# The two ends of a state-space mixer: ScalarE's tables behind the outputs, the last gelus and weights behind the last outputs, three steps for the gated unit's first tiles, three more idle products

## The chip, the cores and the metric

One core of a Trainium2 chip runs the whole step in one launch. The metric is the device time of one execution in microseconds (us); smaller is better. Engines are named as in the profile: PE (TensorE's products), DVE (VectorE), ACT (ScalarE), POOL (GpSimd), SP (the engine whose queue issues most transfers). "1.2 GHz" and "2.4 GHz" are the two levels of TensorE's granted clock, 0.50 and 1.00 in the profile's column PEclk.

## The reference

Two layers over 1024 prompt frames and 64 sample frames, 1024 wide, float32. Layer 0 is windowed attention with a gated convolution behind it, layer 1 the state-space mixer with a gated convolution behind it. Only the mixer and what joins it matter here:

```python
u = h.reshape(b, n_blk, blk, N_GROUPS, GROUP_SIZE)          # h = rms_norm(x), 64 groups of 16
xr, xi = einsum('blgi,gpi->blgp', u, bbr), einsum('blgi,gpi->blgp', u, bbi)
_, _, sr, si = lax.associative_scan(_affine_combine, (ar, ai, xr, xi), axis=1)
y = einsum('blgp,gip->blgi', sr, cr) - einsum('blgp,gip->blgi', si, ci)
y = y + d_skip * h
z = gelu(y)
ag = z @ w_glu + b_glu                                       # 1024 -> 2048, the gated unit
out = ag[..., :D_MODEL] * sigmoid(ag[..., D_MODEL:])
x = x + rms_norm(out, g_post)
```

## The kernel before

**The mixer's loop** (`ssm`, L1190 to L1355). The 64 groups are 32 pairs. A batch holds two pairs (the first two and the last two batches hold one), 18 batches in all. A batch goes through four stages, a generator each, and `staged(..., oldest=True)` steps four batches at once, the oldest first. Stage 1: PE multiplies the inputs `U` by the pair's weights `pm` into PSUM tile `p1` (L1243); ACT makes two tables that DVE will need, `sc` (L1251, sines with both signs) and `rd` (L1253, decay times a mask). Stage 2: DVE forms the scan's input from `p1`, the cosines in `pm` and `sc` (L1270, L1275, L1276). Stage 3: DVE scans with `rd` (L1287) and turns the result back (L1290, L1291). Stage 4: PE adds the output products into PSUM tiles `p3` (L1299 from `U`, L1305 from the scan); ACT copies them to `ys` (L1313) and the last states to `fin` (L1316). `p3` has four buffers, two batches' worth; `rd` has two, so the next but one table waits for a scan.

**Column tiles.** Four pairs make one column tile `kt` of 128 channels, eight in all. When its `ys` is full, ACT's queue writes it to memory (`yd`, L1320), SP reads it back transposed (`yf`, L1325), ACT takes the gelu (`z`, L1334 and L1337) and rounds it (`zh`, L1343), DVE forms the remainder (`zl`, L1347). The gelu is held behind the outputs issued so far (`order`, a hint to the scheduler that adds no semaphore). Gelus of tiles 0 to 6 come two further steps after the transfer, that of tile 7 comes at once.

**Weights.** `split_unit` (L211) splits a loaded 128x1024 weight tile into `whl`: ACT rounds it (L214), DVE forms the remainder (L215). The gated unit's weights are loaded ahead through two `raw` buffers, two units ahead of use. u1 to u6 below are the first six: u1 and u2 are needed by its first three tiles, u3 and u4 by the next three, u5 and u6 after that.

**The gated unit** (L1383 to L1411). A tile is (m, b): output columns m, frame block b of 384, 384 and 320 frames. It needs `pb` and `pa`, each 8 column tiles of three products (`mm3`, L218). `pb` and `pa` lie in PSUM where the loop's tiles lay, so the first product waits until ACT has read the last `p3`. Each tile is one generator with two steps: the products of column tiles 0 to 6, then column tile 7, the sigmoid and the gate. The first three tiles (m = 0) all take their first step, then their second. `beside()` runs behind each step and prepares sums of the next layer's weights (`sj`, L1365 to L1373, transfers on POOL's queue).

**The loop's beginning.** `ssm_norm` for the last block forms the norm of its frames; `fill` (L224) keeps PE at work there with products that nobody reads, named `idle` (L1147).

What stands where on an engine is set by a scheduler from program order and the hints of `order`; the rows under "The change" are its result.

Of the kernel before, what the change touches and what calls it, by code (L numbers as in the profile page):

```python
# [8 lines left out]
F32 = mybir.dt.float32  # L9
F32R = mybir.dt.float32r  # L10
I32 = mybir.dt.int32
AF = mybir.ActivationFunctionType
# [3 lines left out]
P = 128  # L16
D = 1024
KD = 8
# [22 lines left out]
OW, OKT, OC, OCO, OSI, PRM = 0, 256, 512, 768, 906, 1044  # L41


class Core:
# [133 lines left out]
    def load_unit(self, src):  # L178
# [30 lines left out]
        return self.split_unit(raw)  # L209

    def split_unit(self, raw):  # L211
        nc = self.nc
        w = self.big([P, 2, D], "whl")
        nc.scalar.activation(w[:, 0], raw, AF.Copy)  # L214
        nc.vector.tensor_sub(w[:, 1], raw, w[:, 0].bitcast(F32))  # L215
        return w
# [17 lines left out]
    def rstd(self, src, n, tag, root, bcast=True, first=False, alt=None, adder=None, fine=False):  # L234
        nc = self.nc
        adder = adder or nc.vector
        acc = None
# [24 lines left out]
        for i, c in enumerate(cuts):  # L262
            nc.tensor.matmul(st[:, i:i + 1], acc[:, 0, c:c + P], self.ones, start=True, stop=True)
        v = self.small.tile([P, 4, 4], F32, name="nv" + tag, bufs=3)
# [877 lines left out]
    def ssm_norm(self, xt, b):  # L1142
# [3 lines left out]
        if b == 2:  # L1146
            self.fill(self.mm_ps("idle"), 7, 512, self.last_tr)  # L1147
        ps, r = self.rstd(xt, n, "sqa" if b == 2 else "sqb", True, bcast=b < 2, alt=1 - b % 2, adder=nc.gpsimd if b == 0 else None)
# [12 lines left out]
        if b < 2:  # L1161
            nc.scalar.activation(self.rn[:, 384 * b:384 * b + 384], ps[:, :n], AF.Copy)
            return
        ex = self.ex
        for i, c in enumerate(range(0, n, P)):
            c = min(c, n - P) // 8
            nc.vector.tensor_scalar(ex[:, 16 * i:16 * i + 16], self.dsel, r[:, i:i + 1], None, op0=ALU.mult)
            nc.tensor.matmul(ps[:, c:c + 16], self.lsel, ex[:, 16 * i:16 * i + 16], start=True, stop=True)
        nc.scalar.activation(self.rs[:, 0:32], ps[:, :32], AF.Copy)
# [20 lines left out]
    def ssm(self, after):  # L1190
# [4 lines left out]
        with tc.tile_pool(name="ss", bufs=1) as sp:  # L1195
# [36 lines left out]
            def batch(qs):  # L1232
# [17 lines left out]
                for c in range(2):  # L1250
                    nc.scalar.activation(sc[:, :, c], pm[:, :, OSI:PRM], AF.Copy, scale=(1.0, -1.0)[c])  # L1251
                for e, q in enumerate(qs):
                    nc.scalar.activation(rd[:, e], mask[:, None, :].to_broadcast([P, 2, 138]), AF.Copy, scale=self.rho[:, q:q + 1])  # L1253
                if qs[-1] == 31:
# [63 lines left out]
                if qs[-1] % 4 == 3:  # L1318
# [10 lines left out]
                    if kt < 7:  # L1329
                        yield  # L1330
                        yield
                    z = self.t4([P, T], "z")
                    yv = yf.rearrange("p t c -> p c t")
# [16 lines left out]
            scans, ends = [], []  # L1350
            self.staged([batch(x) for x in [[0], [1]] + [[q, q + 1] for q in range(2, 30, 2)] + [[30], [31]]], oldest=True)
            fo = sp.tile([P, P], F32, name="fo")
            nc.vector.tensor_add(fo, *(fin[:, i].rearrange("p q c s -> p (q c s)") for i in range(2)))
# [30 lines left out]
        with self.boundary():  # L1384
            def tile_(m, b):
                t0, n = BLK[b]
                if m not in ws:
                    ws[m] = self.unit(("w_glu", m)), self.unit(("w_glu", m + KD))
                if m == 0:
                    y[b] = self.bt(self.yp, b, "y")  # L1390
                pa, pb = self.mm_ps("pa"), self.mm_ps("pb")

                def products(ks):
                    for ps, w in ((pb, ws[m][1]), (pa, ws[m][0])):
                        for k in ks:
                            self.mm3(ps[:, :n], w, slice(k * P, (k + 1) * P), zh[b][:, k], zl[b][:, k], k == 0, k == KD - 1)
                products(range(KD - 1))
                yield
# [8 lines left out]

            order = [tile_(m, b) for m, b in self.tail_order(KD, 3)]
            for x in order[:3] * 2 + [x for x in order[3:] for _ in range(2)]:
                next(x)  # L1410
                beside()  # L1411
# [161 lines left out]
```

## Time and profile before

| | us |
|---|---|
| three runs, median (lowest to highest) | 2277.55 (2268.62 to 2286.29) |
| the profiled execution | 2263.99 |
| its span, from first to last instruction | 2262.2 |
| PE busy in the span | 2200.3 (97%) |
| DVE / ACT / POOL busy | 1687.2 / 1019.6 / 418.0 |

The mixer's loop runs from about 1198 to 1305 us of the span; the gated unit follows until about 1508. In the page's 40 slices PE shows 9 nearly everywhere and 8 in the three slices of the loop. A busy PE is not a PE at its peak, since products are pipelined and slower at 1.2 GHz. In the timeline a row gives start, duration, engine, line, operation, tiles, a count (x2 for two alike, merged), and in brackets the idle time of that engine ahead of it with what ended it.

### The profile page before, as it was taken

To read this page: it belongs to the slowest core of one execution; us is meant where nothing else is said; L and a number is where in the kernel's file an instruction comes from. 1 tells how busy PE (TensorE), PEld (TensorE's weight loads), DVE (VectorE), ACT (ScalarE), POOL (GpSimd) and SP (SyncE) were. 2 spreads that over 40 slices of the span, in tenths; PEclk is the share of its full clock that TensorE was granted. 3 is DMA by queue.
4 is the path that set the end of the run, shared out by engine and by line. 5 is a ranking of instruction groups with operands and counts; after the bars stand their busy time and mean duration, and the time that the engine had idled before them with its cause. 6 is when DMAs were issued, how large, how long until landed. Compare 5 with 4: busy or idle time off the path is not lost. (4 is left out here: it accounts for less than half of the span.)

```text
span 2262.2 us, 36054 instructions
## 1 busy us (share of the span) xinstructions
PE 2200.3 (97%) x13869; PEld 2125.5 (94%) x13869; DVE 1687.2 (75%) x2954; ACT 1019.6 (45%) x1839; POOL 418.0 (18%) x474
## 2 busy tenths in 40 slices
PE   9999999999999999999998889999999999999997
PEld 8987789999999999999986689999999999999997
DVE  8677647989877877767758845588997787676764
ACT  5255747422333342555545632253544444345543
POOL 5322004200042414000200035352011011100000
PEclk9999999999999999999998899999999999999999
DMA  5100024655345565887649778752266677568772
GB/s 196 37 21 29 14 68 150 240 190 200 121 138 186 185 208 178 269 272 234 232 159 347 250 249 296 262 166 72 87 220 224 227 276 260 201 236 291 230 255 99
DMA packets 208124, 428.48 MB, mean 189 GB/s; under 512 B 23312, under 2 KB 114224, under 8 KB 205008
## 3 DMA queue, kind: packets, MB, share of 16 engines
q1 hardware_dynamic: 175648, 326.56, 43.4%
q0 software_dynamic: 23984, 95.12, 11.5%
q10 hardware_dynamic: 8320, 4.49, 0.8%
q8 instruction: 109, 1.79, 0.3%
q14 instruction: 63, 0.52, 0.1%
HBM read 297.75 MB, written 128.37 MB: 188 GB/s over the span
## 5 line engine op out<-in xcount | busy, mean ns | idle before, releaser
L220 PE MATMUL mm<-hl,whl 128*128 128x384 f32 (+1 forms) x1960 | 645.0, 329 | 5.9 <-DVE u L517 2.9
L222 PE MATMUL mm<-hh,whl 128*128 128x384 f32 (+1 forms) x1960 | 642.4, 329 | 2.3 <-DVE whl L215 2.3
L221 PE MATMUL mm<-hh,whl 128*128 128x384 f32 (+1 forms) x1960 | 643.6, 328 | 0.0
L220 PEld LDWEIGHTS mm<-hl,whl 128*128 128x128 f32 x1960 | 369.5, 189 | 8.6 <-DVE u L517 3.6
L222 PEld LDWEIGHTS mm<-hh,whl 128*128 128x128 f32 x1960 | 369.4, 189 | 2.9 <-DVE whl L215 2.9
L221 PEld LDWEIGHTS mm<-hh,whl 128*128 128x128 f32 x1960 | 369.9, 189 | 0.0
L214 ACT ACTIVATE whl<-raw 128x1024 fp32r<-128x1024 f32 x202 | 212.9, 1058 | 327.3 <-PE mm L222 170.9
L215 DVE TENSOR_TENSOR whl<-raw,whl 128x1024 fp32r<-128x1024 f32 x202 | 255.3, 1268 | 101.1 <-ACT whl L214 98.0
L220 PE MATMUL mm<-gt,whl 128*128 128x384 f32 (+1 forms) x968 | 317.7, 329 | 4.6 <-ACT whl L214 1.8
L222 PE MATMUL mm<-gt,whl 128*128 128x384 f32 (+1 forms) x968 | 316.3, 327 | 0.7 <-DVE whl L215 0.7
L221 PE MATMUL mm<-gt,whl 128*128 128x384 f32 (+1 forms) x968 | 316.5, 327 | 0.0
L220 PEld LDWEIGHTS mm<-gt,whl 128*128 128x128 f32 x968 | 182.3, 188 | 6.1 <-ACT whl L214 2.1
L222 PEld LDWEIGHTS mm<-gt,whl 128*128 128x128 f32 x968 | 182.1, 188 | 1.0 <-DVE whl L215 1.0
L221 PEld LDWEIGHTS mm<-gt,whl 128*128 128x128 f32 x968 | 182.4, 189 | 0.0
L194 DVE TENSOR_TENSOR whl<-raw,whl 128x1024 fp32r<-128x1024 f32 x84 | 94.7, 1134 | 72.0 <-ACT whl L193 71.3
L193 ACT ACTIVATE whl<-raw 128x1024 fp32r<-128x1024 f32 x84 | 82.6, 987 | 123.6 <-DMA raw<-sd 55.0
L416 ACT ACTIVATE t<-u,ppt 128x1090 f32<-128x1090 f32 x88 | 114.2, 1298 | 49.8 <-DVE u L518 25.1
L417 DVE SCALAR_TENSOR_TENSOR t<-u,ppt,t 128x1090 f32<-128x1090 f32 x88 | 123.6, 1407 | 8.4 <-ACT t L416 7.8
L418 DVE SCALAR_TENSOR_TENSOR t<-u,ppt,t 128x1090 f32<-128x1090 f32 x88 | 123.4, 1403 | 0.4
L408 DVE TENSOR_TENSOR u<-rb,mm 128x384 f32<-128x384 f32 (+1 forms) x164 | 80.3, 503 | 20.7 <-PE mm L222 16.0
L328 POOL TENSOR_TENSOR y<-y,xl 128x768 f32<-128x768 f32 (+1 forms) x16 | 30.7, 1918 | 349.0 <-DVE y L325 285.6
L560 DVE TENSOR_TENSOR gt<-gr,gt 128x768 fp32r<-128x768 f32 (+2 forms) x106 | 90.4, 881 | 5.6 <-ACT gt L559 5.1
(390 smaller groups left out, 4180.4 us busy)
## 6 DMA issues: line engine op xcount, KB each, us to landing
raw<-in_w_up SPq DMA_DIRECT2D x88, 512.0 KB, 4.2
raw<-in_w_down SPq DMA_DIRECT2D x74, 512.0 KB, 4.3
raw<-sd SPq DMA_DIRECT2D x40, 512.0 KB, 4.3
sj<-in_w_up POOLq DMA_DIRECT2D x68, 256.0 KB, 6.1
su<-sj POOLq DMA_DIRECT2D x34, 512.0 KB, 5.9
raw<-su SPq DMA_DIRECT2D x34, 512.0 KB, 4.8
pm<-prm SPq DMA_DIRECT2D x32, 522.0 KB, 7.1
gr<-td SPq DMA_DIRECT2D x40, 384.0 KB, 6.0
```

What stands on the lines that cost most here:

```text
L193: nc.scalar.activation(w[:, 0], raw, AF.Copy)
L194: nc.vector.tensor_sub(w[:, 1], raw, w[:, 0].bitcast(F32))
L214: nc.scalar.activation(w[:, 0], raw, AF.Copy)
L215: nc.vector.tensor_sub(w[:, 1], raw, w[:, 0].bitcast(F32))
L220: nc.tensor.matmul(out, w[:, 0, sl], xl, start=start, stop=False)
L221: nc.tensor.matmul(out, w[:, 0, sl], xh, start=False, stop=False)
L222: self.last_mm = nc.tensor.matmul(out, w[:, 1, sl], xh, start=False, stop=stop)
L408: nc.vector.tensor_mul(u[:, t0 + 2:t0 + 2 + np_], rb[:, t0:t0 + np_], ps[:, :np_])
L416: nc.scalar.activation(t, u[:, 0:T + 2], AF.Identity, bias=cb(m), scale=cw(0, m))
L417: nc.vector.scalar_tensor_tensor(t, u[:, 1:T + 3], cw(1, m), t, op0=ALU.mult, op1=ALU.add)
L418: self.last_conv = nc.vector.scalar_tensor_tensor(t, u[:, 2:T + 4], cw(2, m), t, op0=ALU.mult, op1=ALU.add)
L560: nc.vector.tensor_sub(x[:, 1, u], raw, x[:, 0, u].bitcast(F32))
```

## The change

Five edits; the arithmetic on the data stays as it is:

1. Each `sc` and `rd` is ordered behind the output copy issued last (`out[0]`), in program order that of three batches earlier.
2. `split_unit` can be ordered: after the loop `behind` holds the last output copy (for ACT's half) and the last L1291 (for DVE's half). It holds for the four units that are split until m = 1 is opened, u3 to u6.
3. Column tile 6 takes one more step between transfer and gelu, column tile 7 two, so both gelus fall behind the last output copies.
4. The m = 0 tiles take three steps: column tiles 0 to 5, then 6, then 7. All three take the first step before anything else, without `beside()`.
5. Eight instead of seven idle products of 512 columns ahead of the norm's sums, one more of 512 behind them (`last_st`), and one of 256 behind the three `sel` products.

```diff
+    behind = ()
     def split_unit(self, raw):
-        nc.scalar.activation(w[:, 0], raw, AF.Copy)
-        nc.vector.tensor_sub(w[:, 1], raw, w[:, 0].bitcast(F32))
+        x = nc.scalar.activation(w[:, 0], raw, AF.Copy), nc.vector.tensor_sub(w[:, 1], raw, w[:, 0].bitcast(F32))
+        for u, v in zip(x, self.behind):
+            self.order(u, v)
...
-            self.fill(self.mm_ps("idle"), 7, 512, self.last_tr)
+            idle = self.mm_ps("idle")
+            self.fill(idle, 8, 512, self.last_tr)
...
+        self.fill(idle, 1, 512, self.last_st)
         for i, c in enumerate(range(0, n, P)):
...
+        self.fill(idle, 1, 256, x)
...
                 for c in range(2):
-                    nc.scalar.activation(sc[:, :, c], pm[:, :, OSI:PRM], AF.Copy, scale=(1.0, -1.0)[c])
+                    x = nc.scalar.activation(sc[:, :, c], pm[:, :, OSI:PRM], AF.Copy, scale=(1.0, -1.0)[c])
+                    if out[0]:
+                        self.order(x, out[0])
                 for e, q in enumerate(qs):
-                    nc.scalar.activation(rd[:, e], ..., AF.Copy, scale=self.rho[:, q:q + 1])
+                    x = nc.scalar.activation(rd[:, e], ..., AF.Copy, scale=self.rho[:, q:q + 1])
+                    if out[0]:
+                        self.order(x, out[0])
...
                     if kt < 7:
                         yield
                         yield
+                    if kt == 6:
+                        yield
+                    if kt == 7:
+                        yield
+                        yield
                     z = self.t4([P, T], "z")
...
+            self.behind = out[0], ends[-1]
...
                     ws[m] = self.unit(("w_glu", m)), self.unit(("w_glu", m + KD))
+                    if m:
+                        self.behind = ()
...
-                products(range(KD - 1))
+                k0 = 0
+                if m == 0:
+                    k0 = KD - 2
+                    products(range(k0))
+                    yield
+                products(range(k0, KD - 1))
                 yield
                 products([KD - 1])
...
+            for x in order[:3]:
+                next(x)
             for x in order[:3] * 2 + [x for x in order[3:] for _ in range(2)]:
```

ACT, the middle of the loop. p3_11901 and p3_11902 are the output of the batch of pairs 8 and 9, sc_11951 and rd_11952 the tables of pairs 14 and 15, sc_12010 and rd_12011 those of pairs 16 and 17. Before:

```order
L1253 ACTIVATE rd_11952<-mask_11569,rho_291 128x276 x2
L1320 DMA yd_11535<-ys_11796 128x8x137
L1334 ACT_TABLE_LOAD
L1334 ACTIVATE z_11888<-yf_11744 128x1024
L1337 ACTIVATE z_11888<-yf_11744 128x64
L1251 ACTIVATE sc_11951<-pm_11745 128x2x138 x2
L1343 ACTIVATE zh_11891<-z_11888 128x384
L1343 ACTIVATE zh_11894<-z_11888 128x384
L1343 ACTIVATE zh_11897<-z_11888 128x320
L1251 ACTIVATE sc_12010<-pm_11801 128x2x138 x2
L1253 ACTIVATE rd_12011<-mask_11569,rho_291 128x276 x2
L1313 ACTIVATE ys_11924<-p3_11901 128x2x137
```

Of the change (the same tiles have numbers higher by 3, lines of the new file: L1323 is the output copy, L1257 `sc`, L1261 `rd`, L1330 `yd`, L1350 `z`):

```order
L1330 DMA yd_11538<-ys_11799 128x8x137
L1350 ACT_TABLE_LOAD
L1350 ACTIVATE z_11891<-yf_11747 128x1024
L1353 ACTIVATE z_11891<-yf_11747 128x64
L1359 ACTIVATE zh_11894<-z_11891 128x384
L1359 ACTIVATE zh_11897<-z_11891 128x384
L1359 ACTIVATE zh_11900<-z_11891 128x320
L1323 ACTIVATE ys_11927<-p3_11904 128x2x137
L1323 ACTIVATE ys_11927<-p3_11905 128x2x137
L1326 COPY fin_11571<-wk_11810 128x8 x2
L1257 ACTIVATE sc_11954<-pm_11748 128x2x138 x2
L1261 ACTIVATE rd_11955<-mask_11572,rho_291 128x276 x2
```

The output copy of pairs 8 and 9 stood behind the tables of both later batches; now it stands ahead of both. This repeats in every round from pairs 8 on.

DVE, the last batches. L1287 (128x552, then two of 128x276) is the scan, L215 a weight split. Before:

```order
L215 TENSOR_TENSOR whl<-raw,whl 128x1024
L1291 TENSOR_TENSOR wk<-wk,sc 128x552
L1270 TENSOR_TENSOR wk<-pm,p_12420 128x2x137
L1275 TENSOR_TENSOR wk<-sc,p_12420 128x2x137
L1276 TENSOR_TENSOR wk<-wk 128x2x137
L1287 SCALAR_TENSOR_TENSOR wk<-rd,wk 128x276
L1290 TENSOR_TENSOR wk<-wk,pm 128x276
L1291 TENSOR_TENSOR wk<-wk,sc 128x276
L1270 TENSOR_TENSOR wk<-pm,p_12471 128x2x137
L1275 TENSOR_TENSOR wk<-sc,p_12471 128x2x137
L215 TENSOR_TENSOR whl<-raw,whl 128x1024
L1276 TENSOR_TENSOR wk<-wk 128x2x137
```

Of the change (L216 is the split, L1301 the old L1291, L1280 the old L1270, L1285 the old L1275, L1286 the old L1276, L1297 the scan):

```order
L1301 TENSOR_TENSOR wk<-wk,sc 128x552
L1280 TENSOR_TENSOR wk<-pm,p_12423 128x2x137
L1285 TENSOR_TENSOR wk<-sc,p_12423 128x2x137
L216 TENSOR_TENSOR whl<-raw,whl 128x1024
L1286 TENSOR_TENSOR wk<-wk 128x2x137
L1297 SCALAR_TENSOR_TENSOR wk<-rd,wk 128x276
L1300 TENSOR_TENSOR wk<-wk,pm 128x276
L1301 TENSOR_TENSOR wk<-wk,sc 128x276
L1280 TENSOR_TENSOR wk<-pm,p_12474 128x2x137
L1285 TENSOR_TENSOR wk<-sc,p_12474 128x2x137
L1286 TENSOR_TENSOR wk<-wk 128x2x137
L1297 SCALAR_TENSOR_TENSOR wk<-rd,wk 128x276
```

One split of the three (u3) has left the last batches; u2's has moved by three instructions and stays among them.

ACT, the hand-over to the gated unit. p_12562 and p_12563 are the last output. Before:

```order
L1334 ACTIVATE z<-yf 128x1024
L1337 ACTIVATE z<-yf 128x64
L214 ACTIVATE whl<-raw 128x1024
L1343 ACTIVATE zh<-z 128x384 x2
L1343 ACTIVATE zh<-z 128x320
L1313 ACTIVATE ys<-p_12562 128x137
L1313 ACTIVATE ys<-p_12563 128x137
L1316 COPY fin<-wk 128x4 x2
L214 ACTIVATE whl<-raw 128x1024
L1320 DMA yd<-ys 128x8x137
L1334 ACTIVATE z<-yf 128x1024
```

Of the change (p_12559 and p_12560 are the last output):

```order
L1323 ACTIVATE ys<-p_12559 128x137
L1323 ACTIVATE ys<-p_12560 128x137
L1326 COPY fin<-wk 128x4 x2
L216 ACTIVATE whl<-raw 128x1024 x2
L1330 DMA yd<-ys 128x8x137
L1350 ACTIVATE z<-yf 128x1024
L1353 ACTIVATE z<-yf 128x64
L1359 ACTIVATE zh<-z 128x384 x2
L1359 ACTIVATE zh<-z 128x320
L216 ACTIVATE whl<-raw 128x1024
L1350 ACTIVATE z<-yf 128x1024
```

The gelu of column tile 6 and one split stood ahead of the last output copy; both now stand behind it, and two splits stand between it and the transfer of column tile 7. On SP's queue the weight load of u6 now stands behind the read-back of column tile 7; before, those of u5 to u8 all stood ahead of it.

## Rows read from the trace of the kernel before

**Rows 1.** Windows: span, PE, PEld, DVE, ACT, POOL busy, clock, DMA share, GB/s.

```profile
1250.00:1260.00 10.00, 9.09 (x107) 7.47 (x106) 9.21 (x13) 5.75 (x19) 0.29 (x2) 1.00 0.75 265
1300.00:1310.00 10.00, 5.34 (x54) 4.26 (x52) 5.57 (x10) 6.90 (x16) 0.00 (x0) 0.84 0.52 166
```

**Rows 2.** Waits of DVE in 1203 to 1292: total us, times, longest.

```profile
DVE zl L1347 <- ACT zh L1343: 5.8, 4, 2.9
DVE whl L215 <- ACT whl L214: 2.0, 1, 2.0
DVE wk L1270 <- ACT fin L1316: 0.5, 2, 0.2
```

**Rows 3.** Waits of PE in the same stretch, same columns.

```profile
PE p L1299 <- ACT ys L1313: 8.2, 5, 2.4
```

**Rows 4.** Timeline of DVE in the loop: two scans, the first wait.

```profile
1214.69 1.31 DVE L1287 TENSOR_TENSOR_SCAN wk<-rd,wk 128x552 f32<-128x552 f32 x1
1219.68 1.31 DVE L1287 TENSOR_TENSOR_SCAN wk<-rd,wk 128x552 f32<-128x552 f32 x1
1238.03 1.03 DVE L1347 TENSOR_TENSOR zl<-z,zh 128x384 fp32r<-128x384 f32 x2 [2.91 <-ACT zh L1343]
```

**Rows 5.** Timeline of all engines, one round of the loop.

```profile
1272.92 2.07 ACT L1334 ACTIVATE z<-yf 128x1024 f32<-128x1024 f32 x1 [0.25 <-ACT fin L1316]
1275.10 0.74 ACT L1251 ACTIVATE sc<-pm 128x276 f32<-128x276 f32 x2
1275.17 1.20 PE L1305 MATMUL p<-wk,pm 64*128 64x137 f32 x16
1278.57 0.94 ACT L1253 ACTIVATE rd<-mask,rho 128x276 f32<-128x276 f32 x2 [1.54 <-DVE wk L1287]
1279.42 0.66 ACT L1313 ACTIVATE ys<-p 128x274 f32<-128x274 f32 x2
1279.85 1.11 PE L1299 MATMUL p<-U,pm 128*128 128x137 f32 x4 [2.39 <-ACT ys L1313]
```

**Rows 6.** Timeline of all engines, the last batches and the hand-over.

```profile
1296.01 1.74 PE L1305 MATMUL p<-wk,pm 64*128 64x137 f32 x12 [0.86 <-DVE wk L1291]
1299.55 1.22 DVE L215 TENSOR_TENSOR whl<-raw,whl 128x1024 fp32r<-128x1024 f32 x1
1304.14 1.20 PE L1305 MATMUL p<-wk,pm 64*128 64x137 f32 x16
1305.68 2.03 ACT L1334 ACTIVATE z<-yf 128x1024 f32<-128x1024 f32 x1 [1.87 <-DMA yf<-yd]
1310.52 0.44 ACT L1313 ACTIVATE ys<-p 128x137 f32<-128x137 f32 x2
1311.00 0.69 PE L220 MATMUL pb<-zl,whl 128*128 128x384 f32 x1 [5.66 <-ACT ys L1313]
```

**Rows 7.** Windows, columns as in Rows 1: the gated unit's first products.

```profile
1311.00:1314.00 3.00, 3.00 (x9) 3.00 (x10) 2.36 (x5) 1.09 (x3) 1.46 (x3) 0.50 0.73 164
1314.00:1324.00 10.00, 10.00 (x58) 10.00 (x57) 0.00 (x0) 0.00 (x0) 3.34 (x5) 0.98 1.06 282
```

**Rows 8.** Timeline of ACT: column tile 7 and the first sigmoid.

```profile
1310.98 0.37 ACTq L1320 DMA_DIRECT2D yd<-ys  x1
1324.68 2.15 ACT L1334 ACTIVATE z<-yf 128x1024 f32<-128x1024 f32 x1 [12.59 <-DMA yf<-yd]
1334.18 0.58 ACT L1402 ACTIVATE sg<-pb,ppt 128x384 f32<-128x384 f32 x1 [4.64 <-PE pb L222]
```

**Rows 9.** Timeline of DVE: the last remainder.

```profile
1327.49 1.43 DVE L1347 TENSOR_TENSOR zl<-z,zh 128x384 fp32r<-128x384 f32 x3 [14.13 <-ACT zh L1343]
```

**Rows 10.** DMA issues in 1200 to 1345: count, KB each, median us to landing.

```profile
pm<-prm SPq DMA_DIRECT2D x26, 522.0 KB, 7.4
yd<-ys ACTq DMA_DIRECT2D x8, 548.0 KB, 8.6
```

**Rows 11.** Timeline of POOL at the loop's beginning.

```profile
1201.65 0.19 POOL L1274 COPY wk<-h 128x2 f32<-128x2 f32 x1 [5.18 <-DMA h<-in_s_h]
```

More of the change, by code (lines that the diff above doesn't have):

```diff
@@ L262, in rstd @@
         for i, c in enumerate(cuts):
-            nc.tensor.matmul(st[:, i:i + 1], acc[:, 0, c:c + P], self.ones, start=True, stop=True)
+            self.last_st = nc.tensor.matmul(st[:, i:i + 1], acc[:, 0, c:c + P], self.ones, start=True, stop=True)
         v = self.small.tile([P, 4, 4], F32, name="nv" + tag, bufs=3)
@@ L1167, in ssm_norm @@
             nc.vector.tensor_scalar(ex[:, 16 * i:16 * i + 16], self.dsel, r[:, i:i + 1], None, op0=ALU.mult)
-            nc.tensor.matmul(ps[:, c:c + 16], self.lsel, ex[:, 16 * i:16 * i + 16], start=True, stop=True)
+            x = nc.tensor.matmul(ps[:, c:c + 16], self.lsel, ex[:, 16 * i:16 * i + 16], start=True, stop=True)
+        self.fill(idle, 1, 256, x)
         nc.scalar.activation(self.rs[:, 0:32], ps[:, :32], AF.Copy)
@@ L1250, in batch @@
                 for c in range(2):
-                    nc.scalar.activation(sc[:, :, c], pm[:, :, OSI:PRM], AF.Copy, scale=(1.0, -1.0)[c])
+                    x = nc.scalar.activation(sc[:, :, c], pm[:, :, OSI:PRM], AF.Copy, scale=(1.0, -1.0)[c])
+                    if out[0]:
+                        self.order(x, out[0])
                 for e, q in enumerate(qs):
-                    nc.scalar.activation(rd[:, e], mask[:, None, :].to_broadcast([P, 2, 138]), AF.Copy, scale=self.rho[:, q:q + 1])
+                    x = nc.scalar.activation(rd[:, e], mask[:, None, :].to_broadcast([P, 2, 138]), AF.Copy, scale=self.rho[:, q:q + 1])
+                    if out[0]:
+                        self.order(x, out[0])
                 if qs[-1] == 31:
```

## The prediction

> **What bounds the kernel now.** Over the whole span PE is busy 97%, so the windows of 10 us show where it isn't: only in the mixer's loop and behind it. In 1250 to 1260 DVE is busy 9.21 of 10 and PE 9.09; in 1300 to 1310 PE is busy 5.34 and DVE 5.57, so there nobody works at the bound [rows 1]. That last stretch and the loop are two different cases, and I read them apart.
>
> *The loop.* The timeline of DVE shows a round: from one scan to the next 4.99 us without a gap [rows 4]. DVE is the pace. What the loop loses is DVE's idle time, and the waits of DVE in 1203 to 1292 name it: 5.8 us, in four pieces, for ACT's `zh` ahead of the remainder `zl`, 2.0 us for ACT's half of a weight split, 0.5 us for `fin` [rows 2]. PE's own wait, 8.2 us for ACT's `ys` [rows 3], is on PE's side and is not added: DVE doesn't stop for it.
>
> Why is ACT late, at 6 busy us in 10? The timeline of one round shows it: `rd` waits 1.54 us for DVE's scan, `ys` stands behind it, and PE waits 2.39 us for that `ys` [rows 5]. ACT works in order. As the order of before shows, the output copy of pairs 8 and 9 stands behind the tables of pairs 16 and 17, and the second `rd` of these can't start before a scan one round later. So outputs, the writes of full column tiles, and the gelus behind them all run about a round late.
>
> *The hand-over.* The loop's last products start at 1304.14 and take 1.20. The last `ys` starts at 1310.52, and the gated unit's first product at 1311.00, after 5.66 us of idle PE. In between ACT waits 1.87 us for the read-back of column tile 6, takes its gelu and splits a weight [rows 6]. None of that is needed for the first product but the last `ys`. Behind the gap PE runs at 1.2 GHz: 9 products in 3.00 us, against 58 in 10 us afterwards [rows 7].
>
> **The change part by part.** The sum is made against the profiled execution, 2263.99 us (span 2262.2). It lies 13.6 below the median of the three runs, 2277.55, so the forecast is the saving taken off the median.
>
> *Tables behind outputs.* Nothing is added on ACT; the copies move ahead. Where does DVE's idle time go?
> - The first `zl` wait, 2.91 us [rows 4], is column tile 0, whose gelu waits for its transfer in either order. Between nothing and 0.6 (the `sc` pair of 0.74 [rows 5] that stood between gelu and `zh` is gone, but `yd` may go out up to 0.6 later): I take 0.3.
> - The other three `zl` waits, 5.8 - 2.9 = 2.9 us, and the 0.5 for `fin` [rows 2]: outputs, writes and gelus come up to a round (5 us) earlier, each wait was under 2 us. Bounds 0 (transfers set the pace instead) and 3.4: I take 3.4.
> - The split of u1 waits 2.0 us [rows 2] behind the gelu of column tile 4, which comes earlier by the same: 2.0, bounds 0 and 2.0.
>
> New waits this could make: `sc` now stands behind `ys` three batches older. From the turned-back scan on, that chain is two runs of L1305 at 1.20 and L1299 between them at up to 1.11, `ys` 0.66, `sc` 0.74 [rows 5]: 4.9 us. DVE needs that `sc` two rounds later, 2 x 4.99 = 10.0 [rows 4]. With a gelu and its `zh` and `zl` in between (1324.68 to 1328.92, 4.2 us [rows 8, 9]) 0.9 us is left. Price taken: nothing.
>
> *Splits behind the last outputs.* The split of u3, 1.22 us on DVE, stood in the last batches, and PE waited there for DVE (0.86 in one row) [rows 6]. It now follows the last batch: 1.1 us, since DVE's neighbouring rows overlap by about 0.1; bounds 0 and 1.2. The splits of u2 and u1 stay. What is late next: u3 and u4 are needed by the second three tiles, over 20 us later; no cost.
>
> *Gelus 6 and 7 behind the last `ys`.* The 5.66 us of idle PE [rows 6] shrink to what lies between `ys` and the first product, 1311.00 - 1310.52 = 0.5: a saving of 5.1, bounds 4 (`ys` itself waits for one more copy) and 5.2.
>
> *The clock.* Without that gap the first ten products should run at 2.4 GHz: 3.35 us shrink to 10 x 0.172 = 1.7 [rows 7], 1.6 saved. Bounds 0 (PE still pauses between the last batches, 0.86 us and more [rows 6], and could enter the gated unit at the slow level) and 1.6; as the loop's last products at 1304.14 run 16 in 1.20, as fast as in the loop's middle [rows 5, 6], I take 1.6. The Trainium skill ("TensorE: Matmul & The Clock Gate", Part 1: The HAM clock gate) says that the slow level is the default and that activity lifts it; the trace agrees, 0.50 behind the gap and 0.98 in the next window. By that rule alone the extra idle products would also be worth something, as follows.
>
> *Idle products.* They fill PE's pauses around the last norm. Little can come of it: the loop's first sum waits for POOL's copy of the start state, which waits for its transfer until 1201.65 [rows 11], whatever PE does. Bounds: 0.5 lost (a 512-column product at the slow level ahead of the `sel` products) and 0.5 gained: I take 0.
>
> *Three steps for m = 0.* PE does 3 x 36 products before it needs column tile 6 and 3 x 6 more before 7: 126 x 0.172 = 21.7 us of cover from the hand-over on, as many as before. Column tile 7's way, from the issue of `yd` to its gelu, takes 1324.68 - 1310.98 = 13.7 us, and to the end of the last `zl` 4.2 more [rows 8, 9]: 17.9. Its `yd` goes out 0.1 to 2.5 us after the hand-over now, as two splits stand ahead of it on ACT (about 1.1 each). So it is ready after 18.0 to 20.4, before the cover ends at 21.7; no cost, upper bound 4 if the transfers land late. On SP the read-back now stands ahead of u6's load; u6 is needed by the third three tiles, some 30 us later.
>
> Sum: 0.3 + 3.4 + 2.0 + 1.1 + 5.1 + 1.6 = 13.5 us saved. Profiled: 2264.0 - 13.5 = 2250.5. From the median: 2277.6 - 13.5 = 2264.
>
> **The rivals.**
>
> *Only the hand-over gains* (2270). The loop keeps its pace because transfers set it: `pm` loads take 7.4 us and `yd` writes 8.6 to land at the median [rows 10], and the gelu waits for both legs of a column tile's way. For it: column tile 0's gelu does wait for its transfer. Against it: the DMA share is 0.75 in 1250 to 1260 [rows 1], so there is room. Saved are 1.1 + 5.1 + 1.6 = 7.8. The Trainium skill ("DMA: Bandwidth & Descriptors", Issuing engines are not separate DMA queues) says that transfers of all queues run on the same 16 engines and interleave; that is a rule against this change, as an earlier `yd` on ACT's queue then takes its bandwidth from SP's `pm` loads. The rows show neither.
>
> *Column tile 7 becomes the wait* (2268). The weight sums' transfers start with the hand-over too and collide with `yd`. If the way takes 4 us more than the margin, PE stands idle 4 us before its last 18 products: 13.5 - 4 = 9.5 saved. Before, sg started 5.3 us after the last `zl` ended (1327.49 + 1.43) [rows 8, 9], so the way had room; now the margin is 1.3 to 3.7.
>
> *Tables become the wait, slower* (2288). In rounds with a gelu 0.9 us is left between `sc` and DVE's use of it. If the read-back lands over 0.9 us after ACT gets to the gelu, ACT stands, and now `ys`, `sc` and `rd` stand behind it. At 6 column tiles inside the loop and 4 us each that is 24 us against 13.5; it turns slower than before at 0.9 + 13.5/6 = 3.2 us of delay per tile. For it: the one such wait that rows show, 1.87 us [rows 6]. Against it: writes go out earlier as well, so read-backs land earlier.
>
> **How the numbers follow.** Chances: forecast 0.57, only the hand-over 0.23, column tile 7 0.15, tables 0.05. All but the last lie between 2264 and 2270. The runs of before spread from 2268.62 to 2286.29, some 9 us to either side, which is wider than the cases; the saving's own bounds run from 4 (clock, loop and u3 all at nothing) to 15. So the range is 2246 to 2281: 2264 less 18 (a low run, the profiled execution was 13.6 under its median, and a full saving), and 2270 plus 11. About 1% is what a measurement of this kernel can tell from no change, 22.8 us here; the forecast is 0.6%. Faster by more needs the saving and a low run together: 0.17. Slower by more needs the tables' case at its worst: 0.03. The rest, 0.80, lies within.
>
> **What would show it.** Right: the wait of the gated unit's first product under 1 us and its first ten products at 2.4 GHz; DVE's waits for `zh` in the loop at about 2.6 us in one piece; no wait of PE for `ys` inside the loop; the last scan-to-scan distance shorter by one split; the first sigmoid about 13 us earlier. Wrong: new waits of DVE's L1275 for `sc`, of ACT's `z` for the read-back in most rounds, or of PE for `zl` before its last 18 products of m = 0.

## The result, and the profile of the changed kernel

The changed kernel took 2260.79 us at the median of six runs (2254.65 to 2264.88), the kernel before 2276.97 in six (2268.62 to 2286.29): a ratio of 0.9929, with a 95% interval from 0.9902 to 0.9956. Two further measurements of the same kernel gave 0.9951 (0.9937 to 0.9964) and 0.9939 (0.9922 to 0.9955). By medians these are 16.2, 12.2 and 15.3 us saved. The forecast was 13.5.

The three intervals stand for 10.0 to 22.3, 8.2 to 14.3 and 10.2 to 17.7 us saved. All of them hold the forecast, none holds "only the hand-over" (7.8), and one holds the rival with column tile 7 (9.5). Which part of the change gave how much has to be read from the traces.

The two profiled executions laid side by side don't show it: the span of before was 2262.2 us, that of the change 2263.1. They are single executions, and the stages that the change doesn't touch differ by more than the saving. The mixer has to be read on a clock of its own. I start it at ScalarE's copy of the last block's norm (`sel`, 128x8), behind which the loop begins. Timeline of ACT, before:

```profile
1198.26 0.16 ACT L1170 ACTIVATE sel<-pr 128x8 f32<-128x8 f32 x1
```

and of the change, with the first sigmoid:

```profile
1203.50 0.16 ACT L1176 ACTIVATE sel<-pr 128x8 f32<-128x8 f32 x1
1330.80 0.58 ACT L1427 ACTIVATE sg<-pb,ppt 128x384 f32<-128x384 f32 x1 [5.07 <-PE pb L225]
```

The change reached the mixer 5.24 us later; in its two further executions `sel` came at 1200.02 and 1196.23, in the second one of before at 1206.20, so this is scatter. From `sel` to the first sigmoid it took 1330.80 - 1203.50 = 127.30 us, before 1334.18 [rows 8] - 1198.26 = 135.92: 8.6 us less. With the further profiled executions of both kernels (the runs e1, e2 and e12 below), cut at the same five places:

| us | before | before, e1 | change | change, e2 | change, e12 | mean saved |
|---|---|---|---|---|---|---|
| `sel` to first scan | 4.38 | 4.09 | 4.09 | 4.14 | 4.24 | 0.1 |
| first to last scan | 99.33 | 101.76 | 95.89 | 95.17 | 93.53 | 5.7 |
| last scan to last products | 2.17 | 2.32 | 3.94 | 2.32 | 2.20 | -0.6 |
| last products to gated unit | 6.86 | 7.35 | 1.75 | 2.01 | 2.13 | 5.1 |
| its first product to first sigmoid | 23.18 | 23.17 | 21.63 | 21.68 | 21.63 | 1.5 |
| sum | 135.92 | 138.69 | 127.30 | 125.32 | 123.73 | 11.9 |

The terms of the forecast were 6.8 for the loop with u3's split, 5.1 and 1.6. The mixer's own clock shows 11.9 us saved on the mean; where the timed runs show more, the rows don't say where it comes from. The 3.94 of the change's first execution is the clock. Timeline of PE, and the window behind its first row with the columns of [rows 1]:

```profile
1297.59 0.51 PE L1315 MATMUL p<-wk,pm 64*128 64x137 f32 x4 [2.05 <-DVE wk L1300]
```

```profile
1298.27:1305.22 6.95, 6.95 (x39) 5.66 (x39) 6.64 (x14) 4.33 (x9) 0.41 (x3) 0.51 0.99 235
```

Behind 2.05 us without work PE ran the last batches at 1.2 GHz (0.51), without a gap, so that its products set the end there. In e2 and e12 most of these products ran at 2.4 GHz, in e2 behind a pause as long (2.06 us), and the way took 2.2 to 2.3 us. The slow form isn't a single case: it came again in e5 and e9 (3.53 and 3.82 us).

**The hand-over.** Timeline of the change, PE and ACT, where [rows 6] showed 5.66 us of idle PE:

```profile
1307.42 1.20 PE L1315 MATMUL p<-wk,pm 64*128 64x137 f32 x16
1308.65 0.46 ACT L1323 ACTIVATE ys<-p 128x137 f32<-128x137 f32 x2 [1.56 <-PE p L1315]
1309.17 0.44 PE L223 MATMUL pb<-zl,whl 128*128 128x384 f32 x1 [0.55 <-ACT ys L1323]
```

The last copy now waits for nothing but its products, and the gated unit starts 0.55 us behind it. The windows behind, with the columns of [rows 7]:

```profile
1309.17:1312.17 3.00, 3.00 (x17) 3.00 (x18) 2.18 (x3) 3.00 (x5) 0.55 (x1) 1.00 0.71 199
1312.17:1322.17 10.00, 10.00 (x60) 10.00 (x59) 3.41 (x6) 6.64 (x11) 4.25 (x6) 1.00 0.87 247
```

The granted clock is 1.00 (2.4 GHz) from the start, where it was 0.50; 17 products fit into 3 us, where it was 9.

**Column tile 7.** ACT and DVE of the change:

```profile
1319.10 2.14 ACT L1350 ACTIVATE z<-yf 128x1024 f32<-128x1024 f32 x1 [1.73 <-DMA yf<-yd]
1321.90 1.43 DVE L1363 TENSOR_TENSOR zl<-z,zh 128x384 fp32r<-128x384 f32 x3 [3.27 <-ACT zh L1359]
```

The last remainder ends at 1321.90 + 1.43 = 1323.33, 14.2 us after the first product. In PE's timeline the first product of column tile 7 starts at 1330.07, 20.9 us after the first product, behind 126 others (108 come ahead of column tile 6). PE never waited.

**The loop.** Waits of DVE and of PE in 1208 to 1297, the same stretch on the mixer's clock as in [rows 2, 3]:

```profile
DVE zl L1363 <- ACT zh L1359: 7.5, 2, 4.2
```

```profile
PE p L1249 <- DMA pm<-prm: 4.8, 5, 2.1
PE p L1309 <- ACT ys L1323: 0.5, 1, 0.5
```

PE's wait for `ys` is down from 8.2 us to 0.5 (what is left is for `pm` transfers; that wait was 2.1 us before, 4.1 in e1), and DVE no longer waits for the weight split or `fin`. But DVE's wait for `zh`, 5.8 us in four pieces before, is now 7.5 in two. Timeline of DVE:

```profile
1243.53 1.03 DVE L1363 TENSOR_TENSOR zl<-z,zh 128x384 fp32r<-128x384 f32 x2 [3.32 <-ACT zh L1359]
1249.78 1.31 DVE L1297 TENSOR_TENSOR_SCAN wk<-rd,wk 128x552 f32<-128x552 f32 x1
1259.19 1.03 DVE L1363 TENSOR_TENSOR zl<-z,zh 128x384 fp32r<-128x384 f32 x2 [4.19 <-ACT zh L1359]
1260.13 1.30 DVE L1297 TENSOR_TENSOR_SCAN wk<-rd,wk 128x552 f32<-128x552 f32 x1
```

The round of column tile 1 takes 10.35 us from scan to scan. Before it took 7.38. ACT, and then SP's queue, show why:

```profile
1247.13 0.37 ACTq L1330 DMA_DIRECT2D yd<-ys  x1
1256.51 2.04 ACT L1350 ACTIVATE z<-yf 128x1024 f32<-128x1024 f32 x1 [7.72 <-DMA yf<-yd]
```

```profile
1247.57 0.33 SPq L1335 DMA_DIRECT2D yf<-yd  x1
```

The write of column tile 2 goes out at 1247.13, the read-back of tile 1 at 1247.57, and its gelu can start only at 1256.51, 8.9 us later. ACT stands for 7.7 of them, with the next outputs behind the gelu. Before, in the order SP, ACT, ACT, by rows of its timeline:

```profile
1242.57 0.33 SPq L1325 DMA_DIRECT2D yf<-yd  x1
1247.17 0.37 ACTq L1320 DMA_DIRECT2D yd<-ys  x1
1247.58 2.08 ACT L1334 ACTIVATE z<-yf 128x1024 f32<-128x1024 f32 x1 [0.25 <-ACT fin L1316]
```

There the read-back of tile 1 had landed in 5.0 us or less, and the write of tile 2 went out 4.6 us behind it. The read-back itself starts at the same time on the mixer's clock (1242.57 - 1198.26 = 44.3, and 1247.57 - 1203.50 = 44.1); what has moved is the write beside it.

Why doesn't it start earlier? On SP's queue it waits for the write of tile 1 to land. That write, on ACT's queue, before and in the change:

```profile
1231.42 0.37 ACTq L1320 DMA_DIRECT2D yd<-ys  x1
```

```profile
1233.04 0.37 ACTq L1330 DMA_DIRECT2D yd<-ys  x1
```

On the mixer's clock it goes out 3.6 us earlier in the change (29.5 against 33.2), but the read-back follows 14.5 us behind it instead of 11.2. In the further executions this is 13.0 and 13.4 us (e2, e12) against 11.7 (e1). So the earlier write of tile 1 gained next to nothing: its read-back starts 43.4 to 44.1 us behind `sel` in the change, 44.3 and 44.6 before.

### The profile page after: what moved, and what is told of

Read it like the earlier page. It is cut to its first block, busy times and chain, and to the rows that moved or that the text cites. A ratio compares the mean times of both kernels' runs of the same rounds, so it can differ in the third digit from the quotient of the medians.

```text
span 2263.1 us, 36074 instructions
## 1 busy us (share of the span) xinstructions
PE 2201.7 (97%) x13875; PEld 2122.4 (94%) x13875; DVE 1688.5 (75%) x2954; ACT 1019.2 (45%) x1839; POOL 415.2 (18%) x474
## 5 line engine op out<-in xcount | busy, mean ns | idle before, releaser
L216 ACT ACTIVATE whl<-raw 128x1024 fp32r<-128x1024 f32 x202 | 212.9, 1058 | 339.1 <-PE mm L225 176.4
L216 DVE TENSOR_TENSOR whl<-raw,whl 128x1024 fp32r<-128x1024 f32 x202 | 254.4, 1263 | 96.7 <-ACT whl L216 96.2
L223 PEld LDWEIGHTS mm<-gt,whl 128*128 128x128 f32 x968 | 182.9, 189 | 10.5 <-DVE y L613 4.9
L562 ACT ACTIVATE gt<-gr 128x768 fp32r<-128x768 f32 (+2 forms) x106 | 78.3, 771 | 39.5 <-DMA gr<-gd 30.2
```

The costliest lines, as they stand in the source:

```text
L216: x = nc.scalar.activation(w[:, 0], raw, AF.Copy), nc.vector.tensor_sub(w[:, 1], raw, w[:, 0].bitcast(F32))
L223: nc.tensor.matmul(out, w[:, 0, sl], xl, start=start, stop=False)
L562: nc.scalar.activation(x[:, 0, u], raw, AF.Copy)
```

## The experiments

My theory was the prediction's sum, loop included. The rivals: that only the hand-over gains, and a collision of the earlier write with the read-back of tile 1, read from the trace above. The table gives the rounds of the loop, from scan to scan, in which remainders of column tiles 0 to 3 and the split of u1 stand before and in the change; "h" is the fourth round, whose wait for POOL's copy of the start state differs from execution to execution, by up to 2.7 us. A tile whose gelu comes a step later has its remainder in a later round: in e7, e11 and e13 those of tiles 2 and 3 stand close together, hence 5.3 and 7.3 instead of 6.07 twice. The last column is the whole loop, first scan to last.

| us | h | tile 0 | tile 1 | tile 2 | tile 3 | u1 | loop |
|---|---|---|---|---|---|---|---|
| before | 4.99 | 9.06 | 7.38 | 7.36 | 7.61 | 8.84 | 99.33 |
| e1, before again | 4.99 | 9.73 | 7.38 | 7.38 | 8.72 | 9.26 | 101.76 |
| change | 4.99 | 9.48 | 10.35 | 6.07 | 6.07 | 6.00 | 95.89 |
| e2, change again | 6.18 | 7.47 | 10.44 | 6.07 | 6.08 | 6.00 | 95.17 |
| e12, change, third | 5.28 | 8.04 | 9.16 | 6.07 | 6.07 | 5.99 | 93.53 |
| e3, tables alone | 4.98 | 8.34 | 10.02 | 6.07 | 6.07 | 6.00 | 95.35 |
| e4, without tables | 7.65 | 7.95 | 7.36 | 7.75 | 7.61 | 9.45 | 101.38 |
| e5, without idle products | 4.98 | 9.47 | 8.46 | 6.06 | 6.07 | 6.00 | 93.99 |
| e6, gelus 0 and 1 later | 4.98 | 5.32 | 9.32 | 10.51 | 9.35 | 6.00 | 97.91 |
| e7, write 2 later | 4.99 | 9.57 | 6.08 | 5.31 | 7.28 | 6.00 | 91.91 |
| e8, two steps | 7.29 | 6.67 | 10.68 | 6.06 | 6.07 | 6.00 | 95.68 |
| e9, writes 1 and 2 later | 6.98 | 6.07 | 5.31 | 5.71 | 7.28 | 8.26 | 92.81 |
| e11, lean | 6.25 | 6.60 | 6.16 | 5.32 | 7.29 | 6.00 | 90.29 |
| e13, lean again | 4.98 | 7.51 | 6.16 | 5.31 | 7.29 | 6.00 | 89.90 |

### The two kernels again (e1, e2)

> The kernel before once more, for a second profiled execution of it, since the profiled execution of before was 13.6 us under its median and that of the change 4.1 us over its own. Lengths are counted from ScalarE's copy of the last block's norm (`sel`, 128x8). Theory A (the mixer's length is stable, the executions differ elsewhere): first scan to last scan 99.3 us, first product of the gated unit at +112.7, first sigmoid at +135.9, each within 2 us. Theory B (the profiled execution of before had a lucky mixer): the mixer is some 5 to 8 us longer in this one.

> The changed kernel once more, for a second profiled execution and a closer ratio. Theory A (sum of the prediction, loop included): the round in which column tile 1 is taken, 10.35 us from scan to scan in the first profiled execution against 7.38 before, was a chance of transfers; here it is under 8, the first sigmoid is 12 to 13 us earlier than before on the mixer's own clock (+123), ratio about 0.993. Theory B (only the hand-over gains): the round is long again, 9.5 to 11, since the earlier write of column tile 2 takes the bandwidth of the read-back of tile 1; first sigmoid at +127, ratio about 0.996.

The kernel before had a mixer of 138.69 us to the first sigmoid, 2.8 longer than in its first profiled execution and above the 2 us that theory A allowed, short of theory B's 5 to 8. It isn't a constant, but its rounds of tiles 1 and 2 are the same to 0.02 us. The round of tile 1 in the change was long again, 10.44, as theory B said, with the same two transfers beside each other (write at 1242.88, read-back at 1243.83, gelu at 1252.35):

```profile
1252.35 2.03 ACT L1350 ACTIVATE z<-yf 128x1024 f32<-128x1024 f32 x1 [7.81 <-DMA yf<-yd]
```

The first sigmoid came at +125.3 and the ratio was 0.9951, between what the two theories gave.

### Tables alone, and all but the tables (e3, e4)

The edit that e3 makes in the kernel before, and that e4 takes out of the change:

```diff
-                    nc.scalar.activation(sc[:, :, c], ...)
+                    x = nc.scalar.activation(sc[:, :, c], ...)
+                    if out[0]:
+                        self.order(x, out[0])
-                    nc.scalar.activation(rd[:, e], ...)
+                    x = nc.scalar.activation(rd[:, e], ...)
+                    if out[0]:
+                        self.order(x, out[0])
```

> Before with the first edit alone: `sc` and `rd` behind the output copy issued last. Theory A: the loop, first scan to last, is 4 to 6 us shorter than 99.3, ratio 0.9975. Theory B (the earlier write collides with the read-back of tile 1): the round of tile 1 grows by 3 us and the later rounds shrink by 1.3 to 1.5 each, together 2 to 3.5 us shorter, ratio 0.9985 to 0.999. Theory C (tables become DVE's wait): longer than before, ratio over 1.001. The gap in front of the gated unit stays over 5 us in all three.

> The changed kernel without its first edit: `sc` and `rd` stand where they stood before, the rest of the change is kept. Theory A: the hand-over's gain alone is left, 7.8 us with the split of u3, ratio 0.9965, first sigmoid at about +128; the loop's rounds are as before (7.4 us where a column tile is taken). Theory B: nearly the same time as the whole change, within 2 us of it, since the tables brought little.

The tables alone gave 0.9979 (0.9969 to 0.9990), 4.1 us by medians; all the rest gave 0.9967 (0.9952 to 0.9983), 8.2. Multiplied they give 0.9946, near the whole change's 0.9951. So the loop does gain, and "only the hand-over" falls: with the tables alone it takes 95.35 us, 4.0 less than 99.33, at the lower edge of theory A. But the collision of theory B is there too: the round of tile 1 is 10.02 with the tables and 7.36 without, and the later rounds are 6.0 to 6.1 with and 7.6 to 9.5 without. ACT waits for the read-back of tile 1 in e3, and hardly in e4:

```profile
1255.18 2.03 ACT L1338 ACTIVATE z<-yf 128x1024 f32<-128x1024 f32 x1 [7.39 <-DMA yf<-yd]
```

```profile
1256.35 2.07 ACT L1346 ACTIVATE z<-yf 128x1024 f32<-128x1024 f32 x1 [0.25 <-DMA yf<-yd]
```

The gap in front of the gated unit was 4.81 us in e3, less than the 5 that I had set as a floor, and 0.54 in e4. The first sigmoid of e4 came at +132.1 instead of +128, since its h round was 2.7 us longer and its loop as long as that of e1.

### The collision by itself (e7)

```diff
                     kt = qs[-1] // 4
+                    if kt == 2:
+                        yield
                     out.append(nc.scalar.dma_start(yd[...], ys[0]))
```

> The changed kernel with the write of column tile 2 (`yd`) one step later, so that on ScalarE's queue it stands behind the gelu of tile 1, and cannot run beside the read-back of tile 1; tile 2's read-back and gelu come a step later too. Theory A (collision: the earlier write takes the bandwidth of the read-back): the read-back of tile 1 lands in 4 to 5 us instead of 8.9, the round of tile 1 shrinks from 10.0 to 10.4 to about 7.4 or less, loop 2.5 to 3 us shorter. Theory B (the read-back is slow for another reason, as the four `pm` loads issued right behind it): it lands in 8 to 9 us again and the round stays over 9.5.

Theory A. The read-back at 1249.32 has no write beside it now (SP first, then ACT), and lands in 4.8 us:

```profile
1249.32 0.33 SPq L1337 DMA_DIRECT2D yf<-yd  x1
```

```profile
1254.10 2.08 ACT L1352 ACTIVATE z<-yf 128x1024 f32<-128x1024 f32 x1 [3.25 <-DMA yf<-yd]
1254.20 0.37 ACTq L1332 DMA_DIRECT2D yd<-ys  x1
```

The four `pm` loads still follow the read-back directly, so theory B falls. The round of tile 1 takes 6.08, and the loop 91.91. The next pair of transfers meets in its turn (tile 2's read-back 1.3 us behind the write of tile 3, 6.9 us to its gelu), but tile 2's remainder comes a step later here and DVE doesn't wait for it. The windows over the read-back of tile 1 alone, columns as in [rows 1], for the change and for e7:

```profile
1247.57:1256.51 8.94, 8.24 (x96) 6.73 (x94) 7.08 (x11) 1.22 (x5) 0.42 (x3) 1.00 1.08 283
```

```profile
1249.32:1254.10 4.78, 4.78 (x58) 3.89 (x57) 4.57 (x7) 1.53 (x6) 0.23 (x2) 1.00 1.04 333
```

The DMA share is full in both (1.08 and 1.04), but with the write beside the read-back the engines move 283 GB/s against 333. The ratio to before, 0.9941 (0.9922 to 0.9959), lies 0.001 below e2's; the intervals don't separate them. So the traces show what the collision costs in the loop (tile 1's round takes 9.2 to 10.4 us in the change, 6.1 here), and the timed runs don't show that it is won back at the end.

### Removing the waits from the other side (e6)

```diff
-                    if kt == 6:
+                    if kt in (0, 1, 6):
                         yield
```

> The changed kernel with one further step between transfer and gelu for column tiles 0 and 1 too, as tile 6 has it. Theory A (VectorE's two waits for `zh`, 5.6 to 7.5 us in the two profiled executions of the change, are pure loss, since these tiles are needed 50 us later): both waits vanish, the loop is 89 to 91 us from first to last scan against 95.2 and 95.9, the rounds of tiles 0 and 1 take 6.1, ratio to before 0.992 to 0.993. Theory B (the loop is paced by transfers there): the wait comes back as PE's wait for `pm` or VectorE's for `p1`; 0 to 2 us faster than the change, ratio 0.994 to 0.995.

Neither. The loop got longer, 97.91 us, with three rounds of 9.3 to 10.5. The waits of ACT in 1203 to 1335 name a releaser that the change didn't have:

```profile
ACT z L1350 <- DMA yd<-ys: 11.1, 2, 6.0
```

The code gives `ys`, `yf` and `z` five shared buffers. A `yf` that is kept a step longer keeps its buffer, and `z` has to take one that a write (`yd`) is still reading. So ACT waits for a write to land instead of a read-back, and DVE's wait for `zh` rises to 8.9 us. Timed, 0.9953 (0.9936 to 0.9970): neither a gain nor a measurable loss against the change. A sixth buffer was not tried.

### Both early writes later (e9)

Against e7:

```diff
-                    if kt == 2:
+                    if kt in (1, 2):
                         yield
```

> The changed kernel with the writes of column tiles 1 and 2 (`yd`) each one step later, so that neither runs beside the read-back of the tile before it. Theory A (the same collision stands behind the wait for tile 0): the read-back of tile 0, 8.0 and 8.2 us from issue to gelu in the change and with tile 2's write alone later, lands in under 6, VectorE's wait for `zh` of tile 0 (3.3 and 3.4 us) falls below 1.5, the loop is 88 to 90.5 us from first to last scan against 91.9, ratio 0.992 to 0.994. Theory B (tile 0 is slow for the `pm` loads and the inputs around it): its wait stays over 3 us. Theory C (buffers: the five shared ones make the gelu of tile 1 wait for a write to land, as in the run with late gelus for 0 and 1): a new wait of ScalarE's `z` for `yd`, loop over 94 us.

Not settled. The read-back of tile 0 went to its gelu in 6.2 us (1231.36 to 1237.58), ACT waited 0.15 us for it, and no wait for `zh` is among DVE's in 1203 to 1295, which is nearly theory A:

```profile
DVE wk L1286 <- POOL wk L1284: 2.8, 2, 2.1
DVE whl L216 <- ACT whl L216: 2.2, 1, 2.2
```

But DVE came late by itself, since the h round had a wait of 2.1 us for POOL (6.98 us). In e8 the h round was as long (7.29), and there, with the write of tile 1 in its old place, 1.2 us behind the read-back (1231.34), the way to the gelu took 6.2 us as well and DVE waited only 0.51. ACT twice, then DVE, of e8:

```profile
1232.53 0.37 ACTq L1330 DMA_DIRECT2D yd<-ys  x1
1237.49 2.07 ACT L1350 ACTIVATE z<-yf 128x1024 f32<-128x1024 f32 x1 [2.02 <-DMA yf<-yd]
```

```profile
1240.21 1.03 DVE L1363 TENSOR_TENSOR zl<-z,zh 128x384 fp32r<-128x384 f32 x2 [0.51 <-ACT zh L1359]
```

So the write of tile 1 is not shown to be what tile 0 waits for. In e9 the u1 split waits again for ACT (2.2 us, round 8.26): the gelu in front of it starts only 6.3 us behind its read-back (1279.89 to 1286.17), and ACT stands for 3.5 of them. The loop is 92.81, no shorter than e7's. Ratio 0.9948 (0.9931 to 0.9966).

### Idle products, three steps (e5, e8)

In e5:

```diff
-            self.fill(idle, 8, 512, self.last_tr)
+            self.fill(idle, 7, 512, self.last_tr)
-        self.fill(idle, 1, 512, self.last_st)
-        self.fill(idle, 1, 256, x)
```

In e8:

```diff
-                if m == 0:
-                    k0 = KD - 2
-                    products(range(k0))
-                    yield
-            for x in order[:3]:
-                next(x)
```

> The changed kernel with the idle products of before: seven of 512 columns ahead of the norm's sums, none behind them and none behind the `sel` products. Theory A (the prediction's 0): the first scan starts 4.1 to 4.4 us after the copy of `sel` as in all five profiled executions so far, and the ratio to before stays within 0.001 of the whole change's 0.995. Theory B (the clock gains): without the extra products the loop's first products run at the slow level for longer, first scan up to 0.5 us and the whole loop 1 to 3 us later, ratio 0.996 or more. Theory C (the products stand in the way): 0.5 to 1 us faster than the whole change.

> The changed kernel with the m = 0 tiles in two steps again (column tiles 0 to 6, then 7), gelus and splits late as in the change. Theory A (the three steps are what makes the late gelu of tile 6 free): PE waits about 3 us for `zl` of tile 6 in its first tile (it comes to it after 18 products, 3.1 us, and the remainder ends 6.2 us after the first product in the change), the first sigmoid comes 3 us later, ratio 0.0013 above the whole change's. Theory B (the three steps bring nothing): no wait over 0.5 us, same time.

Without the idle products the first scan starts at +4.10 (4.09 to 4.24 with them) and the ratio is 0.9954 (0.9937 to 0.9971). They do lift the clock, 0.81 in the 10 us around the norm's last sums against 0.67, windows of the change and of e5:

```profile
1196.50:1206.50 10.00, 6.87 (x37) 4.26 (x36) 4.43 (x15) 5.22 (x12) 0.99 (x7) 0.81 1.03 356
```

```profile
1195.86:1205.86 10.00, 4.97 (x27) 3.98 (x28) 4.43 (x15) 5.22 (x12) 0.99 (x7) 0.67 1.01 349
```

but nothing that sets the end runs on PE there: from the start of the norm's last sums to `sel`, ahead of the mixer's clock, it took 4.28 us in both. Theory A.

In e8 PE didn't wait either: its only wait in 1300 to 1330 is the 0.5 us for the last `ys`. The scheduler had done the same by itself. After 18 products of `pb`, column tiles 0 to 5, comes `pa`, though the code asks for `pb`'s tile 6 next:

```profile
1307.91 0.33 PE L225 MATMUL pb<-zh,whl 128*128 128x384 f32 x1
1308.09 0.33 PE L223 MATMUL pa<-zl,whl 128*128 128x384 f32 x1
```

Tile 6's remainder ends at 1311.0 there, and no product asked for it earlier. Ratio 0.9952 (0.9934 to 0.9971): theory B, the three steps bring nothing here that these runs can tell.

### Only what pays (e11, e13, e12)

The lean kernel is the change with e5's, e7's and e8's edits together: tables, splits and gelus 6 and 7 as in the change, write 2 later, no extra idle products, two steps.

> Only what the runs so far showed to pay: tables behind outputs, splits and gelus 6 and 7 behind the last outputs, and the write of tile 2 one step later; without the extra idle products and with the m = 0 tiles in two steps. Theory A (these parts carry all of the gain): loop 91.5 to 92.5 us from first to last scan, gap in front of the gated unit 0.5, first sigmoid at +122 after the copy of `sel`, ratio 0.993 to 0.995, not slower than the change (0.9951). Theory B (the three steps or the idle products matter where single runs could not show it): ratio 0.996 or more, or the first sigmoid over 1.5 us later than with them.

> The changed kernel beside the lean one on one chip, to tell whether the collision's 3 to 4 us show in timed runs. Theory A (they do): ratio to before 0.9945 to 0.9955 here, and the lean kernel 0.0010 to 0.0020 below it. Theory B (what the trace shows in the loop is taken back later): both ratios alike within 0.0005.

> The lean kernel again, beside the change on one chip. Theory A: ratio to before 0.9930 to 0.9940, the round of tile 1 in its profile under 6.5 us from scan to scan, where the change has over 8. Theory B: the ratio of the change within 0.0005, with the same short round.

The lean kernel gave 0.9942 (0.9920 to 0.9964) and, beside the change, 0.9932 (0.9917 to 0.9948) against the change's 0.9939 (0.9922 to 0.9955), 2249.98 us against 2250.07 at the median. Its loop is the shortest of all (90.29 and 89.90), the round of tile 1 takes 6.16, and the first sigmoid comes at +120.4 and +120.3, against +123.7 to +127.3. In e11 theory A was reached and passed; in e12 and e13 the two ratios lie 0.0007 apart, which fits neither theory of e12, and e13's theory A holds. So the two parts that it leaves out bring nothing that shows, and it beats the kernel before. Whether it beats the change is open: its mixer is 3.3 to 7.0 us shorter in the traces, but the medians beside each other differ by 0.1. Stages that neither kernel touches moved by several us from execution to execution (`sel` came at 1195.98, 1196.23, 1199.20, 1200.02 and 1203.50 in these five profiled executions).

## Why the prediction was right, and where it was off

- **Total.** 13.5 us forecast; 16.2, 12.2 and 15.3 measured, 11.9 on the mixer's own clock. The mechanism of the hand-over was right, term by term. That the loop came near too is in part luck: one term was far too high and another too low (below). The range, 2246 to 2281, is wide enough to hold the time of before as well (2277), so staying inside it says little.
- **Hand-over.** 5.1 forecast, and 5.1 by the mean of the table's rows; 0.54 to 0.55 us of gap against the 0.5 taken. The gap is 0.54 as well without the tables (e4), without the idle products (e5) and with two steps (e8), and 4.81 with the tables alone (e3): so it is the late gelus and splits that close it.
- **Clock.** 1.6 forecast, 1.5 found. Every kernel with the short gap took 21.6 to 21.7 us from the first product to the first sigmoid. The bound of 0 was no idle worry: in the change's first execution PE did run the last batches at 1.2 GHz behind a pause, and came 1.4 us later to the gated unit for it (5.69 us behind the last scan, 4.33 in the other two), but it was back at 2.4 GHz for the loop's last products.
- **u3's split.** 1.1 forecast. The last round is 3.04 to 3.05 us in the change and 3.99 in e3, which has the tables but not the later split: 0.9.
- **Split of u1 and the later waits.** DVE's waits for `zh` of tiles 2 and 3, for u1's split and for `fin` are gone, as forecast. The rounds shrink by as much as the waits or somewhat more: 1.3 for tile 2, 1.5 to 2.7 for tile 3, 2.8 to 3.3 for u1, where 2.0 was taken.
- **The step that failed** is the one on "the other three `zl` waits", taken at 3.4: "outputs, writes and gelus come up to a round (5 us) earlier". It holds for the issue of the writes, not for what comes back. The write of tile 1 went out earlier but took longer to land, so the read-back of tile 1 started at about the same time as before; and that lost 2.4 to 3.9 us to the write of tile 2, which now ran beside it (7.4, 8.5 and 8.9 us in the three executions against 5.0). Tile 1's round grew by 1.8 to 3.1 us. On the mean the rounds of tiles 1, 2 and 3 gave -2.6 + 1.3 + 2.1 = 0.8 us instead of 3.4; u1 gave 3.1 instead of 2.0 and hid a part of this, so the loop gave 5.7 instead of 6.8. The 0.3 for tile 0 can't be read: with the h round in front of it, it took 14.05 and 14.72 us before, 14.47, 13.65 and 13.32 in the change, and why it waits is open (e9).
- **The signs.** Of those for "right", the first product's wait, its clock and the shorter last round came, and PE's wait for `ys` shrank to 0.5 us; the first sigmoid was 11.9 us earlier, not 13, and DVE's waits for `zh` were 7.5, 5.6 and 4.9 us in two pieces, not 2.6 in one. Of those for "wrong", none was seen on PE or for `sc`, but ACT's `z` waited for the read-back at four of the six gelus in the loop in all three executions (tiles 0, 1, 4 and 5; before at one, in e1 at three). Only the waits at tiles 0 and 1 reached DVE.
- **The rivals.** "Only the hand-over gains" came close to this mechanism, but expected the earlier write to take its bandwidth from the `pm` loads; it was the read-back that DVE ended up waiting for. The `pm` loads took a median of 8.2 to 9.4 us to land in the three executions, 7.4 and 8.5 before, and none of DVE's waits in the loop names them. The Trainium skill's rule ("DMA: Bandwidth & Descriptors", Issuing engines are not separate DMA queues) is that transfers issued by different engines run on the same 16 engines and interleave. The trace agrees with it: 8.9 us for a read-back from SP's queue beside a write from ACT's, 4.8 without it. The rival's price was too high, since only tile 1's round grew. "Tables become the wait" came true in part as well (ACT stood 7.7 us for tile 1's read-back, behind it the outputs), though DVE waited for `zh` and not for `sc`; its counter-argument, that read-backs land earlier because the writes do, was wrong there. "Column tile 7 becomes the wait" did not come: it was ready after 14.2 us instead of the 18.0 to 20.4 that the prediction added up, as its write and read-back took 6.0 and 4.0 us. The cover was 20.9 us, not 21.7, since the products of the block of 320 frames are shorter.
- **Idle products and three steps.** Both put at nothing, both nothing; the reason for the second was another one, the scheduler's own order of the products.

## What to carry to other kernels

Read a stage on its own clock, from an event in front of it, before believing two spans: here two executions with equal spans hid 8.6 us. When work moves earlier on an in-order engine, list the transfers that it issues, and look at which other transfers run at the new time: the gain of three rounds paid for a collision in a fourth. A wait that is moved by keeping a tile longer can come back as a wait for the buffer, as in e6. And when a run removes a wait, look whether something else in it came late by chance, as the h round in e9.

## What the runs showed of the hardware that I had not expected

- The same 548 KB read-back (tile 1's) took 4.8 us without a write beside it (e7), and 7.1 to 8.9 in the six executions (the change's three, e3, e5, e8) in which another column tile's write was issued 0.4 to 1.3 us ahead of it; the DMA engines moved 333 GB/s together without the write and 283 with it (e7 and the change's first execution), at a full share in both cases. Not every write beside a read-back costs as much: in the change's first execution those of tiles 4 and 5, with a write issued 1.8 and 0.8 us behind them, took 4.1 and 4.2 us.
- Three more idle products raised the granted clock around the norm's sums from 0.67 to 0.81 of full speed (e5 and the change), and no event behind moved: `sel` came 4.28 us after the start of the last sums in both, the first scan 4.10 and 4.09 us after `sel`.
